# Seven block products for the down-projection of a decoder layer, on one Trainium2 core

## The chip, the core and the metric

The kernel runs on one core of a Trainium2 chip. The core has five engines with a queue each: TensorE (PE in the profile; its weight loads are PEld), VectorE (DVE), ScalarE (ACT), GpSimd (POOL) and SyncE (SP), which here issues all DMA transfers. Each works through its own queue in the written order and waits on semaphores that other engines or landed transfers raise. The metric is the time of one execution of the whole program, in microseconds (us), less is better.

## The reference

One layer of a decoder over 2048 tokens of 1024 channels: an input projection, four token mixers, an output projection, LayerNorm, and then the feed-forward part, which is what matters here:

```python
x = _layer_norm(ALPHA * x + mix, ln1_w[l], ln1_b[l])
h = jnp.square(jax.nn.relu(x @ w_up[l]))
x = _layer_norm(ALPHA * x + h @ w_down[l], ln2_w[l], ln2_b[l])
```

`w_up` is 1024 x 4096, `w_down` 4096 x 1024, everything float32. `h` is 2048 x 4096.

## The kernel before

**Products in three matmuls.** A float32 operand is split into a high part (`hi`, an ACT copy that rounds to fp32r) and a low part (`lo`, the rest, a subtraction). A product is the sum of hi x hi, hi x lo and lo x hi, so each 128 x 128 by 128 x 512 block costs three matmuls. `split` (from L176) gives every third subtraction to POOL and the others to DVE, by a counter over the whole program. In the profile the copy is line L135, the subtraction L115, the matmul L112.

**Up-projection** (`ffn_up`). It works in two halves of 1024 tokens (`hf`), each in 16 steps `s`. A step makes the blocks of `h` for the rows `s` and `s + 16` of 128 features and both groups of 512 tokens: a 2 x 2 block product, done with seven products P1 to P7 of 12 matmuls (Winograd's form of Strassen's scheme) instead of eight. The sums of the weights are formed per step (`ffn_w`), those of the activations once per half (`ffn_x`, `ffn_x1`). The seven results lie in six PSUM banks in turn and are added up by DVE in four SBUF tiles, `q1`, `u2`, `u3` and `c`; ACT applies Relu and Square, and SP stores each into `HT`, the transposed `h` in DRAM (L1310). Loads of `w_up` are L1268, into five buffers `wr`.

**Between its steps** the up-projection's first half runs the last output tiles of the mixers (`out_final`) and the activations of the second half (`ffn_x1`).

**Down-projection** (`ffn_down`). It takes the 4096 features in 8 chunks `c` of 4 x 128. For each chunk it splits 8 weight tiles of 128 x 512, then goes through all 2048 tokens in 8 blocks `b` of 256, loading two tiles of `h` (four transfers of 128 KB, L1355) and splitting them. Each block makes 4 products (two token tiles, two halves of the columns) of 12 matmuls, in all 8 x 8 x 4 x 12 = 3072. The results are added to the running sums `y2`, which stay in SBUF for all 2048 tokens (L128, one DVE instruction each), and the last chunk is followed by the second LayerNorm (`lnorm2`) and the store of the output.

**What sets the order.** The code is put in order by a scheduler that simulates it: each engine's queue is fixed when the kernel is built, and buffers of a pool are handed out in the order in which that simulation frees them. Splits that wait for a buffer stand in the queue of ACT and DVE like everything else.

## Time and profile before

| | us |
|---|---|
| median of 3 runs | 3143.94 (3140.44 to 3146.38) |
| the profiled execution | 3141.53 |
| its span, first to last instruction | 3139.7 |
| mixers and output projection, until the first matmul of the up-projection | about 1815 |
| up-projection | about 1815 to 2435 |
| down-projection, until its last matmul | about 2435 to 3129 |
| last LayerNorm and store | about 3129 to 3140 |

The mean granted TensorE clock is 0.939 of full speed over the span. Of the chain that ended last, 39% of the span is matmuls into the banks, the feed-forward part almost alone. The page's share of a busy engine counts matmuls up to a modelled end, so that of PE is read together with the number of matmuls in a window.

### The profile page before, as it was taken

The page shows a single profiled execution, that of the slowest core. Times are in us where ns is not written, and L with a number is a line of the kernel's source. Part 1 is how long each engine was busy: PE and PEld are TensorE (multiplying, and loading weights), DVE is VectorE, ACT ScalarE, POOL GpSimd, SP SyncE. Part 2 cuts the span into 40 slices and gives each one's busy share as a digit, 9 for nine tenths or more (in the row PEclk, how much of TensorE's full clock was granted, in tenths as well). Part 3 has the DMA queues.
Part 4 walks back from the last instruction along what each step waited for, and adds up shares of the span by engine and source line. Part 5 has one row for each costly group of instructions (what it writes and reads, how often), then busy time and mean ns, then how long its engine had stood idle before and what let it go on. Part 6 is the DMA issues. An engine that isn't in the chain of part 4 may idle for free. (4 is left out here: it accounts for less than half of the span.)

```text
span 3139.7 us, 45037 instructions
## 1 busy us (share of the span) xinstructions
PE 2966.3 (94%) x15908; PEld 2423.9 (77%) x15908; DVE 1799.8 (57%) x3577; ACT 1167.7 (37%) x2566; POOL 1061.1 (34%) x1115
## 2 busy tenths in 40 slices
PE   7899989989899999899998699999999999999998
PEld 6667777777678788777777578788888888888887
DVE  3457589778877865533455756556544333333338
ACT  3334434433442453333334454455444111111113
POOL 1333366465544645300123733434322111111111
PEclk9899898999898999699898799999999999999999
DMA  5443333333343354443455545535333622222213
GB/s 169 131 118 108 108 97 96 120 105 83 115 108 88 113 167 125 151 138 118 144 172 167 158 147 175 176 127 180 111 111 101 211 74 74 74 77 78 64 54 125
DMA packets 266483, 381.47 MB, mean 121 GB/s; under 512 B 28304, under 2 KB 146192, under 8 KB 266000
## 3 DMA queue, kind: packets, MB, share of 16 engines
q1 hardware_dynamic: 266256, 378.58, 38.1%
q8 instruction: 126, 2.06, 0.3%
q14 instruction: 101, 0.83, 0.1%
HBM read 264.51 MB, written 113.97 MB: 121 GB/s over the span
## 5 line engine op out<-in xcount | busy, mean ns | idle before, releaser
L112 PE MATMUL bank<-x1h,x0h 128*128 128x512 f32 x1024 | 398.3, 389 | 0.0
L112 PE MATMUL bank<-x1l,x0h 128*128 128x512 f32 x1024 | 398.3, 389 | 0.0
L112 PE MATMUL bank<-x1h,x0l 128*128 128x512 f32 x1024 | 398.3, 389 | 0.0
L112 PE MATMUL mm<-xh,wh 128*128 128x512 f32 x672 | 285.3, 427 | 31.2 <-ACT xh L135 19.0
L112 PE MATMUL mm<-xl,wh 128*128 128x512 f32 x672 | 284.5, 424 | 6.0 <-DVE xl L115 3.5
L112 PE MATMUL mm<-xh,wl 128*128 128x512 f32 x672 | 280.6, 418 | 3.2 <-DVE wl L115 3.1
L128 DVE SCALAR_TENSOR_TENSOR y<-y,bank 128x512 f32<-128x512 f32 x176 | 120.4, 686 | 195.6 <-PE bank L112 189.3
L112 PEld LDWEIGHTS bank<-x1h,x0h 128*128 128x128 f32 x1024 | 192.2, 188 | 39.9
L112 PEld LDWEIGHTS bank<-x1l,x0h 128*128 128x128 f32 x1024 | 192.2, 188 | 39.9
L112 PEld LDWEIGHTS bank<-x1h,x0l 128*128 128x128 f32 x1024 | 192.2, 188 | 39.9
L135 ACT ACTIVATE wh<-raw 128x512 fp32r<-128x512 f32 (+1 forms) x220 | 136.6, 630 | 177.0 <-PE mm L112 70.5
L112 PEld LDWEIGHTS mm<-xh,wh 128*128 128x128 f32 x672 | 134.4, 200 | 70.4 <-ACT xh L135 23.2
L112 PEld LDWEIGHTS mm<-xl,wh 128*128 128x128 f32 x672 | 135.2, 201 | 41.2 <-DVE xl L115 7.1
L112 PE MATMUL mm<-wh,xh 128*128 128x256 f32 (+1 forms) x512 | 157.5, 311 | 5.6 <-ACT stg L131 4.1
L135 ACT ACTIVATE x0h<-x0h 128x512 fp32r<-128x512 f32 x64 | 40.3, 630 | 327.8 <-PE bank L112 304.1
L112 PEld LDWEIGHTS mm<-xh,wl 128*128 128x128 f32 x672 | 134.6, 200 | 35.7 <-DVE wl L115 4.2
L115 DVE TENSOR_TENSOR wl<-raw,wh 128x512 fp32r<-128x512 f32 (+1 forms) x146 | 119.9, 826 | 73.4 <-ACT wh L135 65.0
L112 PE MATMUL mm<-wl,xh 128*128 128x256 f32 (+1 forms) x512 | 157.0, 307 | 3.6 <-DVE wl L115 3.6
L112 PE MATMUL bank<-x0h,wh 128*128 128x512 f32 x384 | 152.5, 398 | 7.6 <-DVE c L115 4.2
L112 PE MATMUL mm<-wh,xl 128*128 128x256 f32 (+1 forms) x512 | 154.7, 303 | 0.0
L112 PE MATMUL bank<-x1h,wh 128*128 128x512 f32 x384 | 150.2, 391 | 1.9 <-ACT q L135 1.9
L112 PE MATMUL bank<-x0l,wh 128*128 128x512 f32 x384 | 151.7, 396 | 0.0
(441 smaller groups left out, 7245.4 us busy)
## 6 DMA issues: line engine op xcount, KB each, us to landing
raw<-in_w_ch SPq DMA_DIRECT2D x140, 256.0 KB, 3.0
wr<-in_w_up SPq DMA_DIRECT2D x128, 256.0 KB, 3.2
chF<-stg SPq DMA_DIRECT2D x68, 256.0 KB, 2.4
xraw<-in_xT SPq DMA_DIRECT2D x64, 256.0 KB, 3.7
HT<-u SPq DMA_DIRECT2D x64, 256.0 KB, 3.4
xr<-in_w_down SPq DMA_DIRECT2D x64, 256.0 KB, 3.1
x0h<-HT SPq DMA_DIRECT2D x128, 128.0 KB, 2.5
x0l<-HT SPq DMA_DIRECT2D x128, 128.0 KB, 2.5
```

Source lines behind the costliest of these rows:

```text
L112: return self.nc.tensor.matmul(out, lhsT, rhs, start=start, stop=stop)
L115: (self.nc.gpsimd if eng == "g" else self.nc.vector).tensor_tensor(out, a, b, op=op)
L128: self.nc.vector.scalar_tensor_tensor(out, a, s, b, op0=op0, op1=op1, **kw)
L135: self.nc.scalar.activation(out, in_, AF.Copy)
```

## The change

The down-projection becomes a 2 x 2 block product by seven products too. Per half of the tokens, a step takes 4 x 128 features of the first 2048 and the 4 x 128 that lie 2048 further on, 128 tokens of the first 512 and 128 of the second 512 (`p` = 0 to 3), and both halves of the columns. Each product is 12 matmuls into one bank. Four chunks `v` of features times four `p` times two halves are 32 steps.

- The activations that the products need are, for P1, P2 and P4, blocks of `h`, and for P3, P5, P6, P7 sums of them. The up-projection forms the sums at the end of each step (two on DVE, two on POOL) and stores seven tiles per step where it stored four, into `H7`, in rows of 512 bytes, so that a later load is one transfer of 256 KB.
- The sums of the weights (P4 to P7) are formed by the new `ffn_t`, 16 times, beside the up-projection, and kept in DRAM (`TD`).
- `u2` gets a second buffer, and `wr` has four instead of five.
- In the down-projection the running sums are kept for one half of the tokens only (16 tiles of 128 x 512), and all weights are loaded and split once per half. The products' weights change in different steps: `OFF` shifts P1 and P6 by one step, P2 and P4 by two, P5 and P3 by three, so that P1 and P6 change in the steps 0, 4, 8, ... at their end, P2 and P4 one step later, P5 and P3 two, P7 three.
- The results pass through sums in SBUF: t = P1, u2 = t + P6, u3 = u2 + P7; t, u2 and u3 are added to the running sums by POOL, P2, P3, P4 and P5 by DVE.

```diff
-        self.HT = [self.dp.tile([P, self.seq], F32, name=f"HT{f}") for f in range(FF // P)]
+        PN = [f"P{n}" for n in range(1, 8)]
+        self.H7 = [{n: [self.dp.tile([P, 4, 4, P], F32, name=f"H{hf}{n}_{c}") for c in range(4)] for n in PN} for hf in range(2)]
+        self.TD = {n: [self.dp.tile([P, 512], F32, name=f"TD{n}_{f}") for f in range(16)] for n in ("P4", "P5", "P6", "P7")}
...
-            raw = self.t(fw, "wr", [P, 512], bufs=5)
+            raw = self.t(fw, "wr", [P, 512], bufs=4)
...
-        def out(f, l, r):
+        def relu2(r):
             self.act(r, r, AF.Relu)
             self.act(r, r, AF.Square)
-            t0 = 1024 * hf + 512 * l
-            self.nc.sync.dma_start(self.HT[f][:, t0 : t0 + 512], r)
...
+            def out(n, r):
+                self.nc.sync.dma_start(self.H7[hf][n][s // 4][:, :, s % 4, :], r.rearrange("p (q t) -> p q t", q=4))
...
             self.add("v", u2, u2, prod(W, "P3"))
-            out(s, 1, u2)
+            relu2(u2)
+
+            self.add("v", c22, u2, c22)
+            out("P5", c22)
+            self.sub("g", u2, c11, u2)
+            out("P7", u2)
+            self.sub("v", c11, c22, c11)
+            out("P6", c11)
+            self.sub("g", u3, u3, c11)
+            out("P3", u3)
             between(s)
 
+    def ffn_t(self, f):
+
+        nc, w = self.nc, self.ap["w_down"]
+        b12, t1, b22 = self.raw(w[f][:, 512:]), self.raw(w[f][:, :512]), self.raw(w[f + 16][:, 512:])
+        b21 = self.t(self.of, "x1t", [P, 2, 512], bufs=1)[:, 0]
+        nc.sync.dma_start(b21, w[f + 16][:, :512])
+        self.sub("v", t1, b12, t1)
+        nc.sync.dma_start(self.TD["P5"][f], t1)
+        self.sub("g", b12, b22, b12)
+        nc.sync.dma_start(self.TD["P7"][f], b12)
+        self.sub("v", b22, b22, t1)
+        nc.sync.dma_start(self.TD["P6"][f], b22)
+        self.sub("g", b21, b21, b22)
+        nc.sync.dma_start(self.TD["P4"][f], b21)
...
+    OFF = {"P1": 1, "P6": 1, "P2": 2, "P4": 2, "P5": 3, "P3": 3, "P7": 0}
...
+            def hpair():
+                nh[0] += 1
+                if nh[0] % 8 < 2:
+                    z = self.t(of, "z2", [P, 2, 512], F32R, bufs=2)
+                    return z[:, 0], z[:, 1]
+                return [self.t(fd, x, [P, 512], F32R, bufs=6) for x in ("hh", "hl")]
+
+            def raw(src):
+                nraw[0] += 1
+                r = self.t(*((self.fr, "xr") if nraw[0] % 7 < 3 else (of, "wl")), [P, 512], bufs=3 if nraw[0] % 7 < 3 else 4)
+                nc.sync.dma_start(r, src)
+                return r
...
+            def prod(n, i):
+                ps = self.slot("py", [P, 512])
+                hi, lo = hpair()
+                self.split(raw(self.H7[i // 16][n][chunk(n, i)][:, i % 4].rearrange("p s t -> p (s t)")), hi, lo)
+                for k in range(4):
+                    ks = slice(k * P, k * P + P)
+                    wh, wl = W[n][k]
+                    for m, (x, w) in enumerate(((hi, wh), (hi, wl), (lo, wh))):
+                        self.mm(ps, x[:, ks], w, start=(k == 0 and m == 0), stop=(k == 3 and m == 2))
+                if i + 1 < nsteps and chunk(n, i + 1) != chunk(n, i):
+                    load_w(n, chunk(n, i + 1))
+                return ps
...
+                t, u2, u3 = (self.t(of, "wh", [P, 512], bufs=4) for _ in range(3))
+                self.copy("a", t, prod("P1", i))
+                self.add("v", u2, t, prod("P6", i))
+                both(0, 0, prod("P2", i), t)
+                self.add("v", u3, u2, prod("P7", i))
+                p5 = prod("P5", i)
+                acc(0, 1, p5, last=False)
+                self.add("g", y[0][1], y[0][1], u2)
+                both(1, 1, p5, u3)
+                both(1, 0, prod("P4", i), u3)
+                acc(0, 1, prod("P3", i), first=False)
...
-        B.ffn_up(1, next(X1), lambda s: None)
+        B.ffn_up(0, X, lambda s: run(B.out_final(11 + s)) if 0 < s < 5 else next(X1) if 7 < s < 12 else B.ffn_t(s) if s > 11 else None)
+        B.ffn_up(1, next(X1), lambda s: B.ffn_t(s - 1) if 0 < s < 13 else None)
```

Three places of the queues show what is moved. The first is ACT in the down-projection. Before, at the change from one chunk to the next, copies of weight tiles (`x1h`, from `xr`) stand between those of activations (`x0h`, made in place of what was loaded):

```order
L135 ACTIVATE x0h_3985_22899<-x0l_3984_22896 128x512 [waits DMAHW2_49,DMAHW3_49,DVE_49,PE_49]
L135 ACTIVATE x1h_4024_23353<-xr_4023_23351 128x512 [waits PE_49]
L135 ACTIVATE x1h_4027_23359<-xr_4026_23357 128x512 [waits PE_49]
L135 ACTIVATE x1h_4030_23365<-xr_4029_23363 128x512 [waits PE_49]
L135 ACTIVATE x0h_3988_22958<-x0h_3987_22955 128x512 [waits DMAHW4_49,DMAHW5_49,DVE_49,PE_49]
L135 ACTIVATE x1h_4033_23371<-xr_4032_23369 128x512 [waits DMAHW6_49]
```

Now, in step 8, ACT has four weight tiles of P1 (`x1h`, from `xr` and `wl`), the copy of P1's bank, three weight tiles of P6, then the activations of P2 (`hh_4318`), the fourth weight tile of P6, and the activations of P7 (`hh_4321`):

```order
L135 ACTIVATE x1h_4292_23803<-xr_4291_23801 128x512 [waits DMAHW0_49,PE_49]
L135 ACTIVATE x1h_4295_23809<-wl_4294_23807 128x512 [waits DMAHW5_49,PE_49]
L135 ACTIVATE x1h_4298_23815<-wl_4297_23813 128x512 [waits DMAHW6_49,PE_49]
L135 ACTIVATE x1h_4301_23821<-wl_4300_23819 128x512 [waits DMAHW2_49,PE_49]
L135 ACTIVATE wh_4286_23781<-bank2_63 128x512 [waits Pool_49]
L135 ACTIVATE x1h_4307_23846<-xr_4306_23844 128x512 [waits DMAHW1_49,PE_49]
L135 ACTIVATE x1h_4310_23852<-xr_4309_23850 128x512 [waits DMAHW3_49,PE_49]
L135 ACTIVATE x1h_4313_23858<-xr_4312_23856 128x512 [waits DMAHW6_49,PE_49]
L135 ACTIVATE hh_4318_23869<-wl_4320_23871 128x512 [waits DMAHW7_49,DVE_49]
L135 ACTIVATE x1h_4316_23864<-wl_4315_23862 128x512 [waits DMAHW5_49,PE_49]
L135 ACTIVATE hh_4321_23889<-wl_4323_23891 128x512 [waits DMAHW0_49,Pool_49]
```

The activations of two products stand behind weight tiles that wait for matmuls of the same step. The load into `wl_4320` waits for a DVE instruction, the subtraction that ends P1's second weight tile, that into `wl_4323` for POOL's, which ends the third.

The second place is PE in the same step. Before, a product's 12 matmuls into one bank stand together (weight tiles `x1h` and `x1l`, activations `x0h` and `x0l`):

```order
L112 MATMUL bank1_62<-x1h_4111_23959,x0h_4153_24315 128x512
L112 MATMUL bank1_62<-x1l_4112_23960,x0h_4153_24315 128x512
L112 MATMUL bank1_62<-x1h_4111_23959,x0l_4154_24316 128x512
L112 MATMUL bank1_62<-x1h_4117_23971,x0h_4153_24315 128x512
L112 MATMUL bank1_62<-x1l_4118_23972,x0h_4153_24315 128x512
L112 MATMUL bank1_62<-x1h_4117_23971,x0l_4154_24316 128x512
```

Now, behind the end of P6 (bank 3) come two matmuls of P2 (bank 4), two of P7 (bank 5), and only then the other ten of P2, the first of which needs the low part:

```order
L112 MATMUL bank3_64<-x1l_4145_23141,hh_4303_23826 128x512
L112 MATMUL bank3_64<-x1h_4144_23140,hl_4304_23827 128x512
L112 MATMUL bank4_65<-x0h_4172_23304,hh_4318_23869 128x512 [waits Activation_49]
L112 MATMUL bank4_65<-x0l_4173_23305,hh_4318_23869 128x512
L112 MATMUL bank5_66<-x0h_4267_23698,hh_4321_23889 128x512 [waits Activation_49]
L112 MATMUL bank5_66<-x0l_4268_23699,hh_4321_23889 128x512
L112 MATMUL bank4_65<-x0h_4172_23304,hl_4319_23870 128x512 [waits DVE_49]
L112 MATMUL bank4_65<-x0h_4175_23310,hh_4318_23869 128x512
```

P7's first matmuls are placed ahead of P2's other ones. In most other steps the products stand one after the other. In all, PE's queue has 384 matmuls fewer.

The third place is SP in the third step of the up-projection's second half. Before, a step has eight transfers (`wr` loads, `HT` stores):

```order
L1310 DMA HT2_15375<-q1_3457_19493 128x512 [waits DMAHW5_49,Activation_49]
L1268 DMA wr_3487_19755<-in_w_up 128x512 [waits DMAHW6_49,DVE_49]
L1268 DMA wr_3488_19757<-in_w_up 128x512 [waits DMAHW7_49,DVE_49]
L1310 DMA HT18_15391<-c_3460_19496 128x512 [waits DMAHW0_49,Activation_49]
L1310 DMA HT18_15391<-u3_3459_19495 128x512 [waits DMAHW1_49,Activation_49]
L1268 DMA wr_3509_19901<-in_w_up 128x512 [waits DMAHW2_49,Pool_49]
L1310 DMA HT2_15375<-u2_3458_19494 128x512 [waits DMAHW3_49,Activation_49]
L1268 DMA wr_3510_19903<-in_w_up 128x512 [waits DMAHW4_49,DVE_49]
```

Now it has 26, of which these are the last twelve (`H1..` are stores of the step's seven tiles, `xr`, `x1t` and `TD..` belong to `ffn_t`):

```order
L1270 DMA wr_3516_20097<-in_w_up 128x512 [waits DMAHW3_49,Pool_49]
L1196 DMA xr_3593_20594<-in_w_down 128x512 [waits DMAHW6_49,DMAHW4_49]
L1315 DMA H1P5_0_15417<-c_3480_19790 512x1x128 [waits DMAHW5_49,DVE_49]
L1196 DMA xr_3594_20596<-in_w_down 128x512 [waits DMAHW1_49]
L1359 DMA TDP4_4_15433<-x1t_3568_20427 128x512 [waits DMAHW7_49,Pool_49]
L1196 DMA xr_3595_20598<-in_w_down 128x512 [waits DMAHW2_49,DMAHW0_49]
L1315 DMA H1P7_0_15425<-u2_3478_19788 512x1x128 [waits Pool_49]
L1315 DMA H1P6_0_15421<-q1_3477_19787 512x1x128 [waits DVE_49]
L1270 DMA wr_3541_20264<-in_w_up 128x512 [waits DMAHW3_49,Activation_49,Pool_49]
L1315 DMA H1P3_0_15409<-u3_3479_19789 512x1x128 [waits DMAHW4_49,Pool_49]
L1351 DMA x1t_3596_20600<-in_w_down 128x512 [waits DMAHW7_49,DMAHW5_49]
L1353 DMA TDP5_5_15450<-xr_3594_20596 128x512 [waits DMAHW6_49,DVE_49]
```

The weight sums of `ffn_t` run ahead of the steps that they were written in: twelve of them stand in the first seven steps of the second half (176 transfers), and the last steps of that half have eleven transfers each.

More of the change, by code (lines that the diff above doesn't have):

```diff
@@ L1317, in ffn_up @@
             self.add("v", c11, c11, prod(W, "P2"))
-            out(s, 0, c11)
+            relu2(c11)
+            out("P1", c11)
             p5 = prod(W, "P5")
@@ L1385, in lnorm2 @@
-    def lnorm2(self, t, ys, stat, pool, lns):
+            ys = [self.t(fd, f"y2_{n}", [P, 512]) for n in range(5)]
+            nraw, nh = [0], [0]
+            def hpair():
[9 more added lines that the diff above has]
+                return r
@@ new lines, in ffn_down @@
+            for n in ("P1", "P6", "P2", "P7", "P5", "P4", "P3"):
+                load_w(n, chunk(n, 0))
+                if n == "P6":
+                    lns = self.t(of, "ln1", [P, 2, D], bufs=1)
+                    nc.sync.dma_start(lns, self.ap["lns"][2:4].partition_broadcast(P))
+            self.t(fd, "hh", [P, 512], F32R, bufs=6)
+            self.t(fd, "hl", [P, 512], F32R, bufs=6)
+            ys += [self.t(fd, f"y2_{n}", [P, 512]) for n in range(5, 14)]
+            two = self.t(of, "x1t", [P, 2, 512], bufs=1)
```

97 lines of the change are left out of this document (44 added, 53 removed).

## The prediction

> **What bounds the kernel now.** I read the page first (busy shares, then the chain that ended last), then the windows of the two feed-forward stages, then the groups of the last stage.
>
> ```profile
> PE 2966.3 (94%) x15908; PEld 2423.9 (77%) x15908; DVE 1799.8 (57%) x3577; ACT 1167.7 (37%) x2566; POOL 1061.1 (34%) x1115
> ```
> ```profile
> core 0: us, PE busy (x) PEld busy (x) DVE busy (x) ACT busy (x) POOL busy (x), PEclk, DMA share, GB/s
> 1815.00:2110.00 295.00, 291.94 (x1286) 240.74 (x1286) 171.75 (x246) 149.04 (x264) 108.78 (x77) 0.98 0.47 154
> 2110.00:2150.00 40.00, 38.85 (x171) 31.60 (x169) 30.12 (x39) 24.52 (x45) 18.89 (x14) 1.00 0.69 227
> 2150.00:2440.00 290.00, 290.00 (x1268) 238.03 (x1269) 146.00 (x210) 148.18 (x254) 91.59 (x67) 1.00 0.35 117
> 2440.00:3126.00 686.00, 686.00 (x3028) 568.01 (x3028) 296.71 (x498) 130.95 (x229) 84.25 (x73) 1.00 0.28 91
> ```
>
> The first two lines of stages are the up-projection's first half and its end, the third its second half, the fourth the down-projection. In the fourth, PE is busy in all 686 us at a granted clock of 1.00, while DVE works 43%, ACT 19%, POOL 12%, DMA 28%. PE alone bounds it. One matmul costs 686.00/3028 = **0.2266 us**; the 389 ns of a single one in the next view overlaps its neighbour, so the window's pitch is what counts.
>
> ```profile
> L112 PE MATMUL bank<-x1h,x0h 128*128 128x512 f32 x1024 | 398.3, 389 | 0.0
> L112 PE MATMUL bank<-x1l,x0h 128*128 128x512 f32 x1024 | 398.3, 389 | 0.0
> L112 PE MATMUL bank<-x1h,x0l 128*128 128x512 f32 x1024 | 398.3, 389 | 0.0
> ```
>
> That is 3 x 1024 = 3072 matmuls, with no idle before any group: 3072 x 0.2266 = 696 us.
>
> **What goes.** A step of the new stage makes seven products of 12 matmuls; 32 steps give 32 x 7 x 12 = 2688. So 384 matmuls go: 384 x 0.2266 = **-87.0 us**. A product then lasts 12 x 0.2266 = 2.72 us, a step 84 x 0.2266 = 19.03 us. The up-projection's step has 84 matmuls too.
>
> **What comes, in the down-projection.** Every product needs its own activations split (ACT copy, then a subtract on DVE, each third one on POOL), and weights are split anew for each half of the tokens: 32 x 7 + 56 x 4 = 448 splits where there were 128 + 64 = 192.
>
> ```profile
> L135 ACT ACTIVATE x1h<-xr 128x512 fp32r<-128x512 f32 x72 | 44.8, 630 | 53.7 <-DMA xr<-in_w_down 28.4 <-PE bank L112 23.7 <-POOL xr L115 0.5
> L115 DVE TENSOR_TENSOR x1l<-xr,x1h 128x512 fp32r<-128x512 f32 x38 | 26.2, 692 | 15.2 <-ACT x1h L135 15.0
> L115 POOL TENSOR_TENSOR x1l<-xr,x1h 128x512 fp32r<-128x512 f32 x13 | 16.8, 1293 | 57.5 <-ACT x1h L135 57.5
> L128 DVE SCALAR_TENSOR_TENSOR y<-y,bank 128x512 f32<-128x512 f32 x176 | 120.4, 686 | 195.6 <-PE bank L112 189.3 <-DMA y<-x 6.2
> L115 POOL TENSOR_TENSOR ws<-wr,wr 128x512 f32<-128x512 f32 x32 | 42.8, 1339 | 86.3 <-DMA wr<-in_w_up 55.5 <-issue 15.5 <-DVE wl L115 15.3
> ```
>
> Per step of 19.03 us: ACT 14 x 0.63 + one copy of a bank (0.63) = 9.5 us; DVE 9.33 x 0.69 + 7 adds from PSUM x 0.69 = 11.3; POOL 4.67 x 1.29 + 4 adds x 1.34 (the ws row, the nearest) = 11.4; DMA 14 x 0.262 MB = 3.7 MB, 193 GB/s. Each fits under PE, so by rates the extra work is hidden; its price lies where a queue waits.
>
> **The reload wait.** In every fourth step P1 and P6, neighbours, change their weights. ACT's queue then has P1's four weight copies, each behind the matmuls that last read its tile, and P2's activations are loaded into a buffer freed by one of them.
>
> ```profile
> xr<-in_w_down SPq DMA_DIRECT2D x48, 256.0 KB, 3.1
> y<-x SPq DMA_DIRECT2D x22, 256.0 KB, 5.5
> ```
> ```profile
> xr<-x1T SPq DMA_DIRECT2D x7, 256.0 KB, 4.4
> ```
>
> The first two are from the window 2440 to 3126 (91 GB/s), the third from 2105 to 2150 (217 GB/s). Count from P6's start, P1 having ended at 0. P1's second weight tile is free at -2.72 + 6 x 0.2266 = -1.36; copy to -0.73, subtract to -0.04; the load of P2's activations lands at about 3.1; copy to 3.7. PE was through with P6 at 2.72: 1.0 us idle. PE does two matmuls (0.45) and then, in its written order, two of P7, whose load waited for a POOL subtract (-0.68 + 0.63 + 1.29 = 1.24), lands at 4.4 and is copied by 5.0: another 0.8. With small gaps 2.0 us a site. The landing is the term: 2.0 at 3.1 us, 3.3 at 4.4, 4.4 at 5.5. I take 2.6 (193 GB/s lies near the 217 row) x 8 sites = **+21** (10 with everything a little earlier, 35 at 5.5).
>
> **The second site.** In the steps after those, P3's activations get a buffer freed by a weight of P2: 2.72 + 0.63 + 1.29 + 0.3 = 4.9 after P2's start, landing 8.0, two copies and a subtract 10.0; P3 is due 4 x 2.72 = 10.9. At 4.4 us the cover is just gone, at 5.5 it lacks 1.3. I take 0.75 x 8 = **+6** (0 to 16).
>
> **Entry and end.** The first steps load 16 y tiles beside weights, as now (y lands at 5.5), so the first reload site costs more: **+4** (0 to 10). At the end both token tiles of the last step wait for its last product; now the next to last is normalised under matmuls.
>
> ```profile
> 3129.33 0.69 DVE L128 SCALAR_TENSOR_TENSOR x0l<-x0l,bank 128x512 f32<-128x512 f32 x1 [0.51 <-PE bank L112]
> ...
> 3135.53 0.75 DVE L128 SCALAR_TENSOR_TENSOR x0l<-x0l,stat,ln 128x512 f32<-128x512 f32 x1
> ```
>
> Four more normalising passes (0.75 each) are then behind the last matmul: **+3** (0 to 5).
>
> **The up-projection.** Each of 32 steps gets two DVE and two POOL sums and three more stores, and 16 weight preparations (two DVE, two POOL sums, four loads, four stores) go beside it; the written order packs twelve of them into the first seven steps of the second half. PE has no gap there now (290.00 of 290.00) and is a step ahead in weights.
>
> ```profile
> 2239.43 1.30 POOL L115 TENSOR_TENSOR ws<-wr,wr 128x512 f32<-128x512 f32 x1 [5.02 <-DVE wl L115]
> 2240.81 1.80 POOL L115 TENSOR_TENSOR wr<-wr,wr 128x512 f32<-128x512 f32 x1
> ...
> 2260.36 1.30 POOL L115 TENSOR_TENSOR wr<-wr,wr 128x512 f32<-128x512 f32 x1
> ```
> ```profile
> 2237.11 0.68 DVE L115 TENSOR_TENSOR c<-u,bank 128x512 f32<-128x512 f32 x1
> ...
> 2240.76 0.69 DVE L115 TENSOR_TENSOR ws<-ws,wr 128x512 f32<-128x512 f32 x1 [1.45 <-POOL ws L115]
> ...
> 2260.58 1.64 DVE L115 TENSOR_TENSOR ws<-ws,wr 128x512 f32<-128x512 f32 x1
> ```
>
> These show one thing more: a DVE sum of two SBUF tiles beside a POOL sum makes one of them late (1.64 for 0.69, or 1.80 for 1.30). Count the two as one resource. A step now needs 2.33 x 1.3 + 2 x 1.3 on POOL and 6.67 x 0.69 on DVE = 10.2 us; the new sums add 2 x 1.3 + 2 x 0.69 = 4.0, a weight preparation as much. Seven steps with twelve preparations: 7 x 14.2 + 12 x 4.0 = 147 in 7 x 19.03 = 133. The 14 us of overload stand against a step of lead, so part of them reaches PE: **+8** (0 to 30).
>
> [...]
>
> **Sum.** -87 + 21 + 6 + 4 + 3 + 8 = -45. The profiled execution took 3141.53 us (span 3139.7), 2.4 us under the median of 3143.94, which is no difference here. 3141.5 - 45 = **3096.5, so 3096**.
>
> **Rivals.**
> 1. The waits are covered: loads land sooner or PE finds other work. Sum -87 + 5 to 20: about 3065 (3058 to 3084). For it: PE's full windows now. Against: the load that waits for a weight's subtract. Chance 0.21.
> 2. DVE with POOL, and DMA, decide: landings of over 4.4 us at all sites (26 + 12), entry 8, the whole overload of 14, end 3: -87 + 63 = 3117 (3112 to 3138). For it: 25 transfers of 0.262 MB in each of the seven full steps are 344 GB/s, and the fullest window here has 227. Against: nobody waits at once for what those steps load. Chance 0.14.
> 3. **Slower**, by one chain in the up-projection. u3 is a single buffer; it is written after P7, ends in the last subtract of the step and its store, and must land before the next P7.
>
> ```profile
> 2254.53 0.69 DVE L115 TENSOR_TENSOR u<-u,bank 128x512 f32<-128x512 f32 x1 [1.53 <-PE bank L112]
> ...
> 2259.97 0.69 DVE L115 TENSOR_TENSOR u<-u,bank 128x512 f32<-128x512 f32 x1 [2.03 <-PE bank L112]
> ...
> 2266.90 0.69 DVE L115 TENSOR_TENSOR u<-q,bank 128x512 f32<-128x512 f32 x1 [3.00 <-DMA HT<-u]
> ```
>
> These are P7, P3 and a wait for such a store today. From P3's add to the next P7's: 19.03 - 5.44 = 13.6 us. Two adds, Relu and Square (1.3), a subtract, POOL's subtract: 0.69 + 1.3 + 0.69 + 0.69 + 1.3 = 4.7, issue 0.4; 8.5 are left for landing and queues. It decides from there: 10.4 stretch a step by 1.9, and 32 x 1.9 = 60 plus the 34 of the down-projection pass the gain by 0.2%; 11 give 32 x 2.5 = 80, 3168. Against it: landings of at most 5.5 so far. Chance 0.13, 0.04 of it within 0.2%.
>
> That the change does not do what it says is out: PE's written order has 384 matmuls fewer.
>
> **Chances and range.** Forecast (3084 to 3112) 0.52, rivals 0.21, 0.14, 0.13. Under 0.2% (6.3 us) cannot be told from no change. Faster: 0.52 + 0.21 + 0.12 = 0.85; same 0.02 + 0.04 = 0.06; slower 0.09. The range, 3064 to 3138, leaves the fastest part of rival 1 (0.05) and rival 3 (0.13) out.
>
> **What would show it.** In the down-projection's window PE's pitch stays 0.2266 and its idle time stands before matmuls on x0 weights with releaser ACT (hh), about 2 to 3 us in every fourth step, some 30 us in all; a step between is 19.0 us. In the up-projection's second half the first seven steps are longer than 19.0 by a microsecond or so and the last ones are not. The forecast is wrong if PE waits in most steps (rival 2), if DVE's wait before u3 for H7's store passes PE's lead (rival 3), or if the clock in these windows falls below 1.00.

## The result, and the profile after

The changed kernel takes **3277.31 us** (median of four runs, 3273.36 to 3298.50) where the kernel before takes 3144.06 (3140.44 to 3146.38): a ratio of **1.0437**, 95% interval 1.0397 to 1.0478, 133 us slower. The forecast was 3096. The profiled execution is the longest of the four: its span is 3296.7 us, 157 us over the one before.

The first line of the page, and the windows of the changed kernel (us of the stretch, busy us and instructions of each engine, granted clock, DMA share, GB/s): the packed part of the up-projection (with the last step of its first half), the entry into the down-projection, its 31 step intervals, the end:

```profile
PE 2966.6 (90%) x15524; PEld 2381.6 (72%) x15524; DVE 2161.5 (66%) x3828; ACT 1333.2 (40%) x2878; POOL 1550.9 (47%) x1432
```
```profile
2150.00:2350.00 200.00, 178.20 (x732) 141.94 (x731) 156.96 (x171) 85.71 (x153) 127.05 (x85) 0.95 0.85 271
2486.00:2526.00 40.00, 22.55 (x86) 17.04 (x84) 28.56 (x31) 23.17 (x40) 21.07 (x14) 0.75 0.97 307
2526.58:3268.70 742.12, 653.26 (x2625) 512.65 (x2625) 477.59 (x620) 288.56 (x516) 403.16 (x282) 0.94 0.54 172
3268.70:3296.60 27.90, 12.23 (x53) 9.39 (x51) 21.21 (x42) 7.87 (x20) 9.70 (x9) 0.78 0.26 99
```

PE has the 384 matmuls less and is busy as long as before: busy counts to a modelled end, so matmuls that follow one another 0.42 us apart instead of 0.23 count as busy all the same. The third line says it: 2625 matmuls in 742 us are 0.283 us each, where 0.2266 was the pitch before, and the clock is 0.94 where it was 1.00.

To cut the span into comparable pieces I use the ACT copy that opens each step, that of P1's bank (`q` in the up-projection, `wh` in the down-projection). Rows of the timeline of the changed kernel, then of before, at the first step of each half, the last step of the up-projection, and the first and last of the down-projection:

```profile
1828.65 0.57 ACT L135 ACTIVATE q<-bank 128x512 f32<-128x512 f32 x1
...
2173.09 0.57 ACT L135 ACTIVATE q<-bank 128x512 f32<-128x512 f32 x1
...
2486.32 0.60 ACT L135 ACTIVATE q<-bank 128x512 f32<-128x512 f32 x1 [0.78 <-PE bank L112]
...
2526.58 0.57 ACT L135 ACTIVATE wh<-bank 128x512 f32<-128x512 f32 x1
...
3268.70 0.58 ACT L135 ACTIVATE wh<-bank 128x512 f32<-128x512 f32 x1
```
```profile
1814.15 0.57 ACT L135 ACTIVATE q<-bank 128x512 f32<-128x512 f32 x1
...
2135.97 0.58 ACT L135 ACTIVATE q<-bank 128x512 f32<-128x512 f32 x1
...
2416.58 0.60 ACT L135 ACTIVATE q<-bank 128x512 f32<-128x512 f32 x1 [0.78 <-PE bank L112]
```

| piece | us | against before or against PE's need | predicted |
|---|---|---|---|
| ahead of the up-projection (code unchanged) | 1828.7 | +14.6 | 0 |
| up-projection, first half | 344.4 | +22.6 | } together |
| up-projection, second half (first to last step) | 313.2 | +32.6 | } +8 |
| last step of up to first of down | 40.3 | +21.2 over 19.03 | +4 |
| 31 intervals of the down-projection | 742.1 | +152.2 over 31 x 19.03 | +27 (21 + 6) |
| the end | 28.0 | +1 (what is left of the sum) | +3 |
| 384 matmuls | | -87 | -87 |

The sum is +157. The 14.6 us ahead of the change are scatter: over the profiles below that piece lies between 1806 and 1832 us with the same code. So lengths of pieces are compared here. In the six kernels below that have the up-projection alike (changed, e1, e2, e3, e7, e10) its first half lies between 340.7 and 345.7 us and its second between 310.6 and 313.8, so a difference of 5 us in the first or 3 us in the second is not read as an effect.

What PE waits for in the 31 intervals (engine, what, for whom: us, times, longest):

```profile
PE bank L112 <- ACT hh L135: 59.8, 21, 6.2
PE bank L112 <- ACT z L135: 13.8, 7, 4.2
PE bank L112 <- DVE z L115: 5.7, 4, 2.3
```

`hh` and `z` are high parts of activations. As the prediction said, it is the products with `x0` weights (P2, P7, P5) that wait most, as these groups of the same window show (count, busy us, mean ns, idle ahead and for whom):

```profile
L112 PE MATMUL bank<-x1h,hh 128*128 128x512 f32 x380 | 153.3, 403 | 20.9 <-ACT hh L135 20.9
L112 PE MATMUL bank<-x0h,hh 128*128 128x512 f32 x279 | 118.8, 426 | 39.0 <-ACT hh L135 38.9
```

The copies come late because their loads do. This is the reload in step 8, whose place in the queues is shown ahead of the prediction: SP's issues (start, time until the last of the group is issued), then ACT's copies, then PE:

```profile
2698.44 1.22 SPq L1389 DMA_DIRECT2D wl<-in_w_down  x2
2700.80 0.33 SPq L1389 DMA_DIRECT2D xr<-H0P  x1
2703.03 0.33 SPq L1389 DMA_DIRECT2D xr<-in_w_down  x1
2703.45 0.38 SPq L1389 DMA_DIRECT2D xr<-TDP  x1
2706.42 0.33 SPq L1389 DMA_DIRECT2D wl<-in_w_down  x1
2706.84 0.38 SPq L1389 DMA_DIRECT2D xr<-TDP  x1
2708.13 0.33 SPq L1389 DMA_DIRECT2D wl<-H0P  x1
2712.93 0.32 SPq L1389 DMA_DIRECT2D wl<-TDP  x1
2714.12 0.32 SPq L1389 DMA_DIRECT2D xr<-TDP  x1
2715.83 1.99 SPq L1389 DMA_DIRECT2D wl<-H0P  x3
```
```profile
2711.55 0.63 ACT L135 ACTIVATE hh<-wl 128x512 fp32r<-128x512 f32 x1 [6.03 <-DMA wl<-H0P]
2712.08 0.61 ACT L135 ACTIVATE x1h<-xr 128x512 fp32r<-128x512 f32 x1
2712.60 1.67 ACT L135 ACTIVATE x1h<-wl 128x512 fp32r<-128x512 f32 x3
...
2719.35 0.63 ACT L135 ACTIVATE hh<-wl 128x512 fp32r<-128x512 f32 x1 [1.65 <-DMA wl<-H0P]
```
```profile
2709.31 0.40 PE L112 MATMUL bank<-x1h,z 128*128 128x512 f32 x1
2712.23 0.50 PE L112 MATMUL bank<-x1h,hh 128*128 128x512 f32 x1 [2.52 <-ACT hh L135]
```

P1's four weight tiles (`in_w_down`) are loaded from 2698.44 on, but they can be copied only as PE goes through P1 of this step, which ends at 2709.5. Two tiles of P6 (`TDP`) follow, and from 2706.84 all seven raw buffers hold weights. The first that comes free takes P6's activations at 2708.13; ACT, which works in order, stands before their copy for 6.03 us, and PE starts P6 only at 2712.23. Behind that copy come P1's weights (2712.08 on). The load of P2's activations waits for the second of these tiles, is issued at 2715.83 and copied at 2719.35. PE, through with P6, starts P2 at 2720.03 (row under "The clock" below). So one reload makes two pauses, of 2.9 and 4.9 us between the starts of matmuls.

The pauses are not in these places alone. Intervals that begin with steps 0, 4, 8, ... take 25.5 us on average, those of the next three steps 25.4, 23.9 and 20.6. Of the 41 pauses of over 0.65 us, 19 (51.5 us beyond the normal pitch) stand within 6 us ahead of and 10 us behind the copy of P1's bank in steps 0, 4, ..., 28; the other 22 (44.3 us) stand elsewhere.

### The profile page after: what moved, and what is told of

It reads as the page before. It is cut to its first block, busy times and chain, and to the rows that moved or that the text cites. A ratio compares the mean times of both kernels' runs of the same rounds, so it can differ in the third digit from the quotient of the medians.

```text
span 3296.7 us, 46483 instructions
## 1 busy us (share of the span) xinstructions
PE 2966.6 (90%) x15524; PEld 2381.6 (72%) x15524; DVE 2161.5 (66%) x3828; ACT 1333.2 (40%) x2878; POOL 1550.9 (47%) x1432
## 5 line engine op out<-in xcount | busy, mean ns | idle before, releaser
L112 PE MATMUL mm<-xh,wh 128*128 128x512 f32 x672 | 283.1, 423 | 30.4 <-ACT xh L135 15.8
L115 POOL TENSOR_TENSOR y<-y,wh 128x512 f32<-128x512 f32 x112 | 165.3, 1486 | 115.8 <-DVE y L128 38.9
L112 PE MATMUL bank<-x0h,wh 128*128 128x512 f32 x384 | 159.1, 415 | 40.7 <-DVE c L115 35.8
L112 PE MATMUL bank<-x1h,hh 128*128 128x512 f32 x384 | 154.8, 403 | 20.9 <-ACT hh L135 20.9
L115 POOL TENSOR_TENSOR wl<-raw,wh 128x512 fp32r<-128x512 f32 (+1 forms) x74 | 103.7, 1402 | 132.5 <-ACT wh L135 114.1
L112 PE MATMUL bank<-x1h,hl 128*128 128x512 f32 x384 | 152.8, 401 | 6.9 <-DVE hl L115 4.8
L112 PE MATMUL bank<-x0h,hh 128*128 128x512 f32 x288 | 122.3, 424 | 39.0 <-ACT hh L135 38.9
L112 PE MATMUL bank<-x0h,wl 128*128 128x512 f32 x384 | 156.1, 406 | 0.0
L112 PE MATMUL mm<-wh,xl 128*128 128x256 f32 (+1 forms) x512 | 154.5, 303 | 0.0
L112 PE MATMUL bank<-x1l,hh 128*128 128x512 f32 x384 | 153.8, 401 | 0.0
L112 PE MATMUL bank<-x1l,wh 128*128 128x512 f32 x384 | 150.7, 393 | 2.2 <-DVE x1l L115 2.1
```

The costliest lines, as they stand in the source:

```text
L112: return self.nc.tensor.matmul(out, lhsT, rhs, start=start, stop=stop)
L115: (self.nc.gpsimd if eng == "g" else self.nc.vector).tensor_tensor(out, a, b, op=op)
```

## The experiments

Theory **A**: raw buffers held by waiting weights starve the activations. Theory **B**: the rates of DVE, POOL and DMA bound the down-projection's step. That sums on DVE and POOL exclude each other is an assumption of B; what the changed kernel's timeline shows is that they lengthen each other (1.77 us for 0.69 and 1.74 for 1.30, rows below). For the up-projection: preparations, stores, buffers or sums. All lengths from the profile of each kernel, us, in the pieces of the table above:

| | half 1 | half 2 | to down | 31 intervals | time |
|---|---|---|---|---|---|
| before | 321.8 | 280.6 | | | 3144.06 |
| changed | 344.4 | 313.2 | 40.3 | 742.1 | 3277.31 |
| e1 late reload | 345.7 | 311.8 | 39.8 | 621.7 | 3159.36 |
| e2 weights split in place | 340.7 | 312.8 | 39.7 | 692.4 | 3224.36 |
| e3 no POOL sums in down | 342.6 | 313.8 | 38.6 | 714.5 | 3247.95 |
| e4 no preparations | 330.8 | 288.7 | 39.5 | 744.0 | 3243.82 |
| e5 long rows | 345.5 | 310.4 | 38.1 | 742.1 | 3297.58 |
| e6 = e1, preparations spread | 335.0 | 322.1 | 54.6 | 621.0 | 3176.94 |
| e7 = e1, entry order | 344.8 | 312.1 | 23.1 | 643.7 | 3162.82 |
| e8 = e6 and e7 | 330.8 | 321.9 | 26.1 | 652.4 | 3174.64 |
| e9 = e1, up sums on DVE | 343.6 | 305.0 | 37.8 | 619.7 | 3152.69 |
| e10 = e1, down sums on DVE | 342.9 | 310.6 | 39.0 | 609.2 | 3147.63 |
| e11 = e9, e10, order of sums | 337.3 | 297.2 | 37.0 | 607.2 | 3129.50 |
| e12 = e11, five raws | 337.8 | 306.9 | 36.4 | 607.9 | 3132.35 |
| e13 = before, four raws | 319.2 | 284.2 | | | 3143.78 |
| e14 = e11, e7, late y | 335.4 | 299.0 | 22.9 | 627.4 | 3128.10 |
| e15 = e12 and e14 | 336.5 | 306.2 | 21.1 | 629.0 | 3142.57 |
| e16 preparations without sums | 334.2 | 291.8 | 39.9 | 736.1 | 3247.87 |
| e17 no step sums in up | 321.5 | 297.4 | 37.5 | 737.1 | 3238.28 |

Times are medians of ten runs for e1, e8, e11 and e15, of four for the first two rows; the others are one run each (thirteen runs of the kernel before, beside e1, reach from 3127.83 to 3163.18).

### The steps of the down-projection

**e1.** The reload is written five products later.

```diff
                 if i + 1 < nsteps and chunk(n, i + 1) != chunk(n, i):
-                    load_w(n, chunk(n, i + 1))
+                    due.append([5, n, chunk(n, i + 1)])
+                for e in due:
+                    e[0] -= 1
+                if due and due[0][0] < 0:
+                    load_w(*due.pop(0)[1:])
```

> The changed kernel with the four loads of a weight reload written five products later (its last user is product j, the loads stand behind product j+5 and not behind product j); everything else, the count of every instruction too, stays. In the changed kernel a step of the down-projection takes 23.9 us on average (31 intervals) where PE needs 19.0. Theory A (the reload line: seven raw buffers are held 15 to 20 us by weights that wait for PE, and the activations' loads queue behind them): the steps fall to 19.0 to 20 us, that is 31 x 4 to 5 us = 120 to 150 us less, about 3140 us. Theory B (rates: DVE, POOL and the DMA cannot do a step's work in 19 us, since sums on DVE and POOL exclude each other): the steps stay above 22.5 us, 3230 us or more.

**e2.** A reloaded weight is split inside its raw buffer and PE does not wait for it.

```diff
-                    load_w(n, chunk(n, i + 1))
+                    for f in range(4 * chunk(n, i + 1), 4 * chunk(n, i + 1) + 4):
+                        r = raw(src(n, f))
+                        self.split(r, r, r)
```

> The changed kernel, but a reloaded weight is split inside its raw buffer (ACT copy, then DVE's or POOL's subtract, both onto the raw tile) and PE goes on with the first weights, so the output is of those weights alone. DMA, ACT, DVE and POOL do all the work they do now; only the wait of the split for PE is gone. Theory A: steps of 19.0 to 20 us. Theory B: steps stay at 22.5 to 24.5 us, since every rate is unchanged.

**e3.** POOL's sums into `y` are left out.

```diff
-                    self.add("g", y[l][j], y[l][j], u)
...
-                self.add("g", y[0][1], y[0][1], u2)
```

> The changed kernel without POOL's four sums into y in each step of the down-projection (left out, so the output lacks three products). POOL loses 4 x 1.49 = 6 us of 11 to 12 us of work a step, and DVE its partner in the shared time. Theory A: the steps stay at 23 to 24 us, since no weight comes free sooner. Theory B: the steps fall by 2 us or more, to below 22.

The windows of the 31 intervals, e1 and then e11 (below):

```profile
2515.59:3137.30 621.71, 611.86 (x2651) 500.27 (x2649) 497.21 (x624) 293.13 (x520) 420.94 (x283) 0.99 0.64 207
```
```profile
2501.23:3108.47 607.24, 600.85 (x2622) 491.59 (x2621) 523.98 (x745) 294.08 (x518) 221.89 (x158) 1.00 0.65 212
```

e1 takes 120.4 us out of the intervals (23.94 to 20.05 us each) and 118 out of the median; the same instructions now run at 207 GB/s, with DVE 80% and POOL 68% busy. So no rate had been the bound: **A holds, B falls** as the main cause. Part of what is left has to do with sums: e10, below, takes another 12.5 us out of the 31 intervals. e3, which takes half of POOL's work away, gives 0.9 us a step; B asked for two.

What e1 changes can be counted. From the issue of a load to the end of the subtraction that frees its buffer, means over 224 loads of activations and 220 of weights (each load followed through the queues by its buffer's name):

```
                 activations  weights   all   buffers in use   14 loads x all / in use
changed              6.4 us    16.6    11.48       6.71              23.96 us
e1 late reload       7.8       11.5     9.59       6.71              20.0
e2 in place         15.2        5.9    10.57       6.70              22.1
e3 no POOL sums      6.2       16.1    11.10       6.75              23.0
```

The seven buffers are nearly always full (6.7 in use), so the step cannot be shorter than 14 loads times the mean stay over seven. That the last column gives the step is bookkeeping; that the step follows when the weights' stay is cut, with all else equal, is e1's evidence. For steps of 19.0 the mean stay may be 9.1 us.

e2 missed: A asked for 19 to 20 us a step and got 22.3, nearer to B's 22.5 to 24.5, so it does not speak for A. There PE waits for something else, banks that DVE has not emptied:

```profile
PE bank L112 <- DVE y L128: 30.6, 25, 3.0
PE bank L112 <- DVE wh L115: 13.4, 12, 2.1
```

DVE's additions from PSUM stand in one queue with subtractions of weights that now come straight from their loads. I read it as a new wait in the old one's place; no run took it away by itself.

### The up-projection

In the up-projection of the changed kernel PE waits for one thing above all, a bank that DVE has not yet added into `c` (us, times, longest); before, this was 4.2 us in two waits:

```profile
PE bank L112 <- DVE c L115: 35.8, 13, 6.2
```

**e4** leaves the calls of `ffn_t` out (the second of the two is shown; the down-projection loads unsummed weights in their place), **e5** stores rows of 2 KB, **e16** leaves out the four sums of `ffn_t`, **e17** the four sums of a step.

```diff
-        B.ffn_up(1, next(X1), lambda s: B.ffn_t(s - 1) if 0 < s < 13 else None)
+        B.ffn_up(1, next(X1), lambda s: None)
```
```diff
-                self.nc.sync.dma_start(self.H7[hf][n][s // 4][:, :, s % 4, :], ...)
+                self.nc.sync.dma_start(self.H7[hf][n][s // 4][:, s % 4], ...)
```
```diff
-        self.sub("v", t1, b12, t1)
...
-        self.sub("g", b12, b22, b12)
...
-        self.sub("v", b22, b22, t1)
...
-        self.sub("g", b21, b21, b22)
```
```diff
-            self.add("v", c22, u2, c22)
...
-            self.sub("g", u2, c11, u2)
...
-            self.sub("v", c11, c22, c11)
...
-            self.sub("g", u3, u3, c11)
```

> The changed kernel without the 16 weight preparations in the up-projection (the down-projection loads four blocks of the weights as they are in the place of the sums, as many bytes). In the changed kernel the up-projection's second half takes 313 us from the first to the last of its 16 steps, before 281, and its first eight steps are the long ones (20 to 26 us). Theory C (the preparations, packed into the first steps, fill DMA, DVE and POOL): the second half comes to 281 to 288 us. Theory D (the chain of the single buffers c and u3 through three more stores a step): it stays above 300 us. The down-projection stays as it is in both.

> The changed kernel with its seven stores a step of the up-projection in 2 KB rows (the down-projection then reads tokens and features mixed, so the output is not the reference's); bytes, sums and preparations stay. In the changed kernel's trace a packet of 512 bytes takes a DMA engine 27 ns, one of 2 KB 84 ns, so four short rows cost 108 ns for 84. In the up-projection's window 2100 to 2300 the short ones are 0.27 of the DMA engines' time. Theory C1 (DMA time decides in the packed steps): the second half (313 us from first to last step, 289 without preparations) falls by 6 us or more. Theory C2 (the sums' engines DVE and POOL and their queues decide): it stays within 4 us of 313.

> The changed kernel without the four sums of each weight preparation (16 x 4 sums left out; it stores the blocks as loaded, so the output is not the reference's); its four loads and four stores stay. The up-projection's halves take 344.4 and 313.2 us with everything, 330.8 and 288.7 without preparations. Transfers cost: both halves stay within 5 us of 344 and 313. Sums cost: the second half falls to 289 to 297, the first to 331 to 338.

> The changed kernel without the four sums in each step of the up-projection (32 x 4 sums left out, the stores keep their number and send the tiles as they are; the output is not the reference's). Shared time: each sum pair of DVE and POOL is 2 us of it, in eight packed steps 8 x 4 us: the second half falls from 313 to 290 to 300. If only the preparations' transfers and their queue decide: it stays above 306.

Without preparations the second half falls to 288.7, 0.7 us above theory C's range and far from D's. Of the 38 us that both halves lose with e4, e16 gives 31.6 by leaving the sums alone out. e17, without the sums of the steps, brings the first half back to 321.5 us, where it was before the change, and the second to 297.4. Both together would be more than the whole loss, so the two groups of sums share it and do not simply add.

The second halves start at different moments, so they are compared from their own first step: the first eight steps of the changed kernel, of e16 and of e4.

```profile
2173.09:2358.70 185.61, 163.97 (x670) 130.22 (x669) 143.28 (x156) 76.71 (x138) 114.50 (x76) 0.94 0.86 276
```
```profile
2149.40:2312.00 162.60, 157.88 (x672) 127.82 (x672) 110.02 (x133) 77.19 (x136) 78.45 (x54) 0.98 0.97 313
```
```profile
2141.50:2296.00 154.50, 149.04 (x641) 120.94 (x640) 113.06 (x132) 77.35 (x138) 75.91 (x53) 0.99 0.58 170
```

e16 moves 313 GB/s with DMA 0.97 busy, more than the changed kernel (276, 0.86), and its eight steps take 162.6 us instead of 185.6; without the transfers too (e4) they take 154.5. So most of the loss is not the transfers; e5's long rows change the second half by 2.8 us, which is within the scatter. **The sums cost.** They stand on two engines whose sums take longer side by side. A piece of the changed kernel's timeline:

```profile
2245.13 1.74 POOL L115 TENSOR_TENSOR x1t<-x1t,xr 128x512 f32<-128x512 f32 x1
2245.64 1.78 DVE L115 TENSOR_TENSOR wl<-wr,wh 128x512 fp32r<-128x512 f32 x1
...
2246.83 1.73 POOL L115 TENSOR_TENSOR u<-q,u 128x512 f32<-128x512 f32 x1
...
2247.34 1.77 DVE L115 TENSOR_TENSOR ws<-ws,wr 128x512 f32<-128x512 f32 x1
```

Side by side a DVE sum takes 1.77 for 0.69 and a POOL sum 1.74 for 1.30. Count both as one resource, DVE sums of two SBUF tiles at 0.684 and POOL sums at 1.29: in the first eight steps of the second half the changed kernel asks for 99 and 75 of them in 668 matmuls, 20.7 us per 84 matmuls; before it was 62 and 37 in 636, 11.9; e4 15.6, e16 14.9, e17 16.3. PE's step is 19.0. This count is an upper estimate: the two pairs above follow one another 1.70 us apart, not 0.684 + 1.29 = 1.97. It orders the runs, but it does not show that the two engines had no time left.

**e6** paces the preparations by a one-column copy from the step's result into each raw tile, **e9** moves the POOL sums of steps and preparations to DVE, **e12** and **e13** exchange a raw buffer (e12 gives back `u2`'s second buffer for it). Of each edit one line is shown.

```diff
+            self.copy("a", r[:, :1], mark[:, :1])
             nc.sync.dma_start(r, src)
```
```diff
-            self.sub("g", u2, c11, u2)
+            self.sub("v", u2, c11, u2)
```
```diff
-            raw = self.t(fw, "wr", [P, 512], bufs=4)
+            raw = self.t(fw, "wr", [P, 512], bufs=5)
```

> The kernel with the late reload, and the 16 weight preparations spread: seven beside steps 5, 6, 7 and 12 to 15 of the first half, nine beside every second step or so of the second half. ACT first copies one column of that step's result into each raw tile, so that its load cannot be written ahead of that step (64 copies of one column are new). In the kernel with the late reload the halves take 345.7 and 311.8 us; without preparations (in the changed kernel) they took 330.8 and 288.7. If it is the packing that costs: the second half falls to 289 to 297 us, the first stays within 335 to 348. If a preparation costs the same wherever it stands (its own 2.5 us or so): the two halves together stay within 8 us of 657.5.

> The kernel with the late reload; in the up-projection the two sums a step and the two sums of a weight preparation that POOL makes are made by DVE. In the changed kernel's trace at 2242 to 2249 a DVE sum of two SBUF tiles beside a POOL sum lasts 1.77 us and POOL's 1.74, where alone they take 0.69 and 1.30: one resource, and a POOL sum costs it 1.30 where DVE would take 0.69. Theory S (this shared time fills the packed steps): 8 x 2 + 12 x 2 sums, each 0.6 us cheaper, take 24 us from the first eight steps of the second half (184 us now); the second half falls from 312 to 288 to 297 us. Theory Q (queues and DMA landings, or DVE by itself, which has 76% busy there): it stays within 5 us of 312, or grows.

> The kernel with all on DVE (e11), with five raw buffers for the up-projection's weights (as before the change) and one buffer for u2 (as before the change) in the place of four and two. With e11 the halves take 337.3 and 297.2 us. Theory R (the raws hold the weights' preparation back): the two fall by 10 us or more together. Theory S (shared time of the packed steps alone): they stay within 5 us.

> The kernel before the change with four raw buffers for the up-projection's weights in the place of five; nothing else. Its halves take 321.8 and 280.6 us. Theory R: longer by 8 us or more together, which is then a term of the change that has nothing to do with sums. Theory S: within 4 us.

e6 did not do what it was meant to: the first half gains 10.7 us, the second loses 10.3, the way into the down-projection 14.8. One interval where the halves meet is 54.4 us: ACT waits 11 us for loads of the second half's activations into `x1t`, a tile that the preparations beside these steps use too. The two halves together come to 657.1 us, which is what the second theory asked for (a preparation costs the same wherever it stands). But the spread brought a wait of its own, so the run does not decide, and what the spread does without that wait was not measured. e9 gains 6.8 us in the second half where Theory S asked for 15 to 24: 17.7 us a step are asked of the shared time in the first eight steps, and they still take 22.1 each. So shared time alone is not the bound. e12 makes the second half 9.7 us longer, against Theory R: there PE waits 17.0 us for DVE's `u`, and DVE 31.7 us for stores of `u` to land, so I read its loss as the price of `u2`'s second buffer, which it gave up. e13 adds 1.0 us to both halves together: the fifth buffer is not the cause. e17 leaves 21.3 us a step in the first eight although it asks for 16.3; what is beyond shared time there stays open.

### The entry

**e7** loads each product's first weights just ahead of its first activations (the loop that loaded all 28 ahead goes), **e14**, built on e11, also loads the `y` tiles of three steps later.

```diff
+                if i == 0:
+                    load_w(n, chunk(n, 0))
                 ps = self.slot("py", [P, 512])
```
```diff
                 self.copy("a", t, prod("P1", i))
+                if i < 3:
+                    load_y(i + 1, t)
```

> The kernel with the late reload, and the first weights of each product loaded just ahead of its first activations, not all 28 ahead of the first activations; the vectors of the last normalisation are loaded in step 8. With the late reload 39.8 us lie between the ACT copies of P1's product in the last step of the up-projection and in the first of the down-projection, where seven products of PE are 19.0: 20.8 us of entry, in one wait of 16 us for the activations of the first product, whose load stands behind 28 weights. Theory E1 (the order of the loads): the gap falls to 22 to 30 us. Theory E2 (the amount: 62 tiles of 0.262 MB at 330 to 390 GB/s take 42 to 49 us whatever their order): what is gained there comes back in the first steps, and gap plus the first four steps (39.8 + 79.7 us now) fall by less than 6 us.

> The kernel with all on DVE (e11) and the entry's order of e7; the y tiles of steps 1, 2 and 3 are loaded behind P1 of the step ahead (ACT writes one column of each from that product first), so 12 of 62 tiles leave the entry. From the last step of the up-projection to the first of the down-projection, and four steps on, took 39.8 + 79.7 us with the late reload and 23.1 + 100.6 in e7; seven products are 19.0, so 24 to 28 us are lost. Amount: 12 x 0.262 MB at 330 to 390 GB/s are 8 to 10 us, gap plus four steps comes to 106 to 113 us. Order alone: it stays at 116 to 124.

With e1 PE has one long wait (15.8 us), for `z` of the first product; so it has in the changed kernel:

```profile
PE bank L112 <- ACT z L135: 16.2, 1, 16.2
```

e7 shortens the gap to 23.1 us and its first interval is 43.7: gap and four intervals come to 123.7 us, against 119.5 with e1 and 113.6 with e11. e14 makes 124.1. The order only moves the wait (e7), as Theory E2 said. But 12 tiles less do not shorten it (e14, where the amount asked for 106 to 113), so the amount of loads is not shown to be the cause either. What decides there (the weight tiles that the up-projection's activations still occupy are the next candidate) was not tried.

### Together

**e10** moves the down-projection's POOL sums to DVE; **e11** adds e9 and another order of the step's sums, P7 over P1, whose store is long done:

```diff
-            self.add("v", c22, u2, c22)
-            out("P5", c22)
-            self.sub("g", u2, c11, u2)
-            out("P7", u2)
-            self.sub("v", c11, c22, c11)
-            out("P6", c11)
-            self.sub("g", u3, u3, c11)
+            self.sub("v", c11, c11, u2)
+            out("P7", c11)
+            self.add("v", u2, u2, c22)
+            out("P5", u2)
+            self.sub("v", c22, c22, c11)
+            out("P6", c22)
+            self.sub("v", u3, u3, c22)
```

> The late reload, the spread preparations and the new order at the entry together. If the three shares add up: 3159 (late reload) less 10 to 20 for the spread and 8 to 18 for the entry, 3125 to 3140 us, under the kernel before. If they share a cause (DMA time that comes back elsewhere): above 3145.

> The kernel with the late reload; POOL's four sums into y in a step of the down-projection are made by DVE. The 31 intervals between its steps take 621.7 us with the late reload, 20.05 each; PE needs 19.0 to 19.2. Theory S: shared time falls from 4 x 1.49 to 4 x 0.69 us a step, the steps fall to 19.2 to 19.7 (595 to 611 us). Theory Q: what is left of the waits is the reload's order and the four y tiles loaded and stored in single steps, and the intervals stay at 617 to 630.

> Both of these, and the four sums of a step of the up-projection in the order P7, P5, P6, P3, with P6 = P4 - P7: P7 goes over P1, whose store is long done, and not P5 over P4, for which DVE waited 21 us on the store's landing (in 13 steps of the changed kernel). Theory S with these waits: 15 to 25 us less in the up-projection, 10 to 25 in the down-projection, so 3159 falls to 3110 to 3135 us, below the kernel before. Theory Q: 3150 us or more.

> e12 and e14 together. Against 3129.5 us of e11: 3105 to 3122 if both theories (raws and amount) hold, 3115 to 3128 if one holds, 3125 to 3140 if neither does.

Ratios to the kernel before, runs on the same chip: e1 1.0036 (1.0003 to 1.0069), e8 1.0088 (1.0055 to 1.0121), e15 0.9997 (0.9973 to 1.0021), and **e11 0.9931 (0.9904 to 0.9958)**: seven products do pay, by 0.7%, once the reload is written later, the sums that POOL made are on DVE and those of a step have another order. In the profiles, from the first step of the up-projection to the end, e11 takes 1305 us and the kernel before 1326. e10 comes to 609 us, inside its range: 19.65 us a step. e11 comes to 3129.5 us, inside its range too, and its pieces also fit Theory S with the store waits: 23 us less than e1 in the up-projection, 14.5 in the 31 intervals. e8 missed its range: the spread had a wait of its own and the entry gave nothing. e15's 3142.57 us lie above all three of its ranges: its two additions give nothing, and the pieces show what each takes, 9 us in the second half, as in e12, and 22 us in the 31 intervals, as in e14, against 16 us gained at the entry.

## Why the prediction was wrong

The forecast was 181 us too low. The right sign stood only in rival 3, and its 3168 was 109 us short, for another cause.

- **What goes.** Right: 2688 matmuls, 87 us; with the waits gone (e11) the intervals are 607.2 us, 31 x 19.6, against 31 x 19.03 expected. The count of splits was a little low, 448 where the trace has 472: six of the seven products start in the middle of a chunk and so load one set of four weight tiles more, 62 sets where 56 were counted.
- **The reload wait, +21, with "the second site", +6.** This is the step that failed: these terms, 27 together, measured 152 us. Place and releaser were right (x0 products waiting for ACT's `hh` around the reload of P1 and P6), and loads landed in 3.5 to 3.7 us (medians of those from `H0` and `H1`), inside the range taken. What was wrong is when the load can be issued. The prediction counted P6 as ready when P1 ended and had P2's load issued at that moment (-0.04), its copy done at 3.7 and PE idle for 1.0 us. In step 8 P1 ends at 2709.5; P6's own activations come 2.7 us late, P2's load is issued 6.3 us after P1's end, and PE waits a second time, 4.5 us. "Each fits under PE, so by rates the extra work is hidden" counted bytes and engine time and left out the **buffers**: seven, for 14 loads a step, and a weight stays 16.6 us in one, mostly because its copy waits for PE's last use of the old tile (5.9 us in e2, where it does not wait for that). The load stood in the order far ahead of that moment. The prediction had the pieces (weights and activations share raw buffers, loads wait for subtractions) and priced one product's wait with all that comes ahead of it on time, not the drain that a reload leaves for the next products: 51.5 us of pauses stand at the eight sites, 44.3 us outside them. e1 shows it: 120 of the 152 us go by the place of a load in the queue.
- **The waits cost more here than their length.** The clock was taken as 1.00, and the prediction named a lower one as a sign of being wrong; it was 0.94. In the 31 intervals 41 pauses of over 0.65 us between matmul starts take 95.7 us beyond the normal 0.2275, and another 230 matmuls start 0.42 us after the one ahead instead of 0.23: 45.4 us more, 40 of it in starts over 0.38 us apart. Together that is 141 of the 152 us; 21 matmuls more in the window than 31 x 84 are another 4.8.
- **The entry, +4.** Measured 21. The first reload was taken as the dear thing; the wait came before it, at the first product. Its cause stays open.
- **The up-projection, +8.** That the sums cost was right, the size was not: 55 us. The number of sums was counted well (147 us in seven packed steps, 21 a step; counted 20.7 in the first eight). What failed is the passage from demand to time: 14 us of overload "against a step of lead" were to vanish by half, whereas the first eight steps of the half take 185.6 us where they had taken 146.8, 39 more. And the first half was not costed at all (+22.6): leaving the steps' own sums out takes all of this back (e17), leaving out the four preparations that stand there 13.6 us of it (e4). By e4, e16 and e17 it is the sums, and not mainly transfers or rows. How they make the step long is open in part: PE waits for DVE's `c`, and moving the sums to DVE (e9) gains 6.8 us in the second half where shared time asked for 15 to 24.
- **The end, +3.** Measured +1.
- **The rivals.** Rival 2 named DVE with POOL and DMA: right for the up-projection as to the engines, not as to DMA (e5, e16), and it gave 3117. Rival 3's chain (a sum that waits for a store to land) exists, over `c` more than `u3`, DVE waiting 21 us and 14 us on them; e9 and e11 differ by that order and, in the down-projection, by e10's sums: their halves of the up-projection differ by 14 us. But such a wait need not cost PE anything: before the change DVE waited 89 us for stores of `u`, and in e4 it waits 36 us for those of `c` while the halves are 38 us shorter. It was neither alone nor the largest. What the prediction said would refute it, "if PE waits in most steps", is what happened: the 31 intervals average 23.9 us, and 28 of them are over 20. It does so for another reason than rival 2's, since e1 runs the same instructions in 20.05 us a step.

## What to carry to other kernels

Beside rates, count buffers: transfers per step times the mean stay of one, over the number of buffers, is a lower bound of the step (here 14 x 11.48 / 7 = 23.0 us of 23.94), and the stay runs to the end of whatever the last reader waits for. A load whose consumer must wait for PE belongs late in the queue, behind the loads that can be used at once (e1: 20.05 us a step for 23.94). And where sums on two engines lengthen each other, as here on DVE and POOL (1.77 us for 0.69, 1.74 for 1.30), try them on the faster one (e9 to e11); do not take spare demand as spare time.

## What the hardware showed

**The clock.** Around a wait of PE in the changed kernel's down-projection (start, us until the modelled end):

```profile
2715.13 0.39 PE L112 MATMUL bank<-x1h,hl 128*128 128x512 f32 x1
2720.03 0.80 PE L112 MATMUL bank<-x0h,hh 128*128 128x512 f32 x1 [4.51 <-ACT hh L135]
2720.62 0.63 PE L112 MATMUL bank<-x0l,hh 128*128 128x512 f32 x1
...
2723.80 0.63 PE L112 MATMUL bank<-x0h,hh 128*128 128x512 f32 x1
2724.23 0.56 PE L112 MATMUL bank<-x0l,hh 128*128 128x512 f32 x1
2724.62 0.39 PE L112 MATMUL bank<-x0h,hl 128*128 128x512 f32 x1
2724.86 0.40 PE L112 MATMUL bank<-x0h,hh 128*128 128x512 f32 x1
```

After 4.9 us without a start the next ten matmuls come 0.39 to 0.60 us apart, then 0.23 again. The granted clock is 0.50 from 2720.0 to 2724.6 and 1.00 from 2724.8 to 2727.0:

```profile
2720.00:2724.60 4.60, 4.57 (x10) 3.32 (x11) 3.35 (x4) 2.66 (x5) 3.20 (x2) 0.50 0.77 222
2724.80:2727.00 2.20, 2.20 (x11) 1.80 (x11) 1.73 (x3) 1.66 (x4) 1.14 (x1) 1.00 1.11 347
```

The slow starts come nearly twice as far apart (0.43 us most of them), and 4.6 us pass from the first of them to the first quick one. In the 31 intervals the ten pauses of 3.15 us or more were all followed by at least seven gaps in a row of 0.33 us or more between starts; those of 2.81 us (from 3196.17), 2.82 (2891.91), 2.83 (3230.84) and 2.91 (2598.43) by seven, one, six and nine, while three of 2.92 to 2.94 us were followed by three. So below 3.15 us the length of a pause alone did not tell how many slow starts came behind it.

**Short rows.** In the changed kernel a packet of 512 bytes takes a DMA engine 27 ns (median, window 2100 to 2300), one of 2 KB 84 ns: four short ones, 108 ns, are 29% dearer. With DMA 0.86 busy long rows (e5) changed the second half by only 2.8 us, which is within its scatter.

**DVE beside POOL.** In the changed kernel's window 2150 to 2350 the 40 DVE additions with a PSUM operand that run beside a POOL sum keep 0.68 us (0.69 at most); the 82 sums of two SBUF tiles that do take 1.40 (median) and up to 1.82, for 0.68 alone. POOL's own sums take 1.67 beside them (median) and 1.29 alone. Counted as one resource, as in the prediction, a pair would ask 0.69 + 1.30 = 1.99 us; the two pairs shown above follow 1.70 us apart. e11, with POOL's sums on DVE and another order of a step's sums, is the quicker kernel (3129.50 us, e1 3159.36) though DVE then works 524 of 607 us in the down-projection.
